# Reordering the attention stretch of a hybrid decoder trunk: feed-forward state opened before the first lead split, and one more weight tile

## The chip, the cores and the metric

The kernel runs on one core of a Trainium2 chip. The time of a kernel is the device time of one launch in microseconds (us), the median of several runs. Engines: PE (TensorE, matrix products and transposes), ACT (ScalarE), DVE (VectorE), POOL (GpSimd), and SP, whose queue issues the loads.

## What is computed

Two decoder layers over 256 tokens of width 1024, batch 1. Each layer is a feed-forward half-step, a token mixer, and a second feed-forward half-step; the first layer mixes with RWKV-7, the second with sliding-window attention over keys and values that are projected once between the layers. The part that matters here is the mixer of layer 1 and what joins it:

```python
D_MODEL = 1024; SEQ = 256; D_FF = 2816; Q_HEADS = 16; KV_HEADS = 4; WINDOW = BLOCK = 128

def swiglu(x, w_in, w_out):
    gate, up = jnp.split(x @ w_in, 2, axis=-1)
    return (jax.nn.silu(gate) * up) @ w_out

# swa_sinks: two query blocks of 128; scores against the previous and the own block of keys
q = (xq @ w_q + b_q).reshape(B, NB, BLOCK, KV_HEADS, GROUP, ATT_HEAD)
s = jnp.einsum('bnqkgd,bnskd->bnkgqs', q, kb) * (ATT_HEAD ** -0.5)
s = jnp.where(valid, s, MASK_VALUE)
p = softmax(concatenate([s, sink]))[..., :-1]
o = jnp.einsum('bnkgqs,bnskd->bnqkgd', p, vb)
return o @ w_o + b_o

# the layer
h = h + 0.5 * rms_norm(swiglu(rms_norm(h, g[0]), ...), g[1])
m = swa_sinks(rms_norm(h, g[2]), ...)
h = h + rms_norm(m, g[3])
h = h + 0.5 * rms_norm(swiglu(rms_norm(h, g[4]), ...), g[5])
```

## The kernel before

All activations stay on the chip; the weights, some 180 MB, are streamed once. Tokens are two halves of 128 (the number 0 or 1 in a unit's name). A weight chunk is 128 x 1024 in float32 (512 KB). `stream` loads it into one of four raw buffers (`wr`), ACT casts it to fp32r (the high part, L195), and DVE subtracts (the low part, L201); a product of two such pairs is three matmuls (`mm3`, L227). The split chunk lies in one of 11 slots in rotation (`W3`, `W1`, `W2`), and waits for the last product that used the slot 11 chunks ago.

The attention stretch is `att_region`. It is written as units, Python generators that emit a few instructions a step; the string `ATT` (L48) is the order in which the steps are taken, and `in_order` ties the instructions of PE, DVE and ACT to that order, each engine by itself. Loads are not tied, and instructions of later parts of the program can be put between by the scheduler. The units:

- `e0`, `e1`: the rest of the previous feed-forward's down projection, four steps of 12 matmuls.
- `p0`, `p1`: norm after it, update of the residual h, statistics; `x0`, `x1`: normed input, transposed in two groups of four (L309), cast and split (L1297, L1299).
- `wq`, `wo`, `wl`: eight steps each, one chunk of the query weights, the output weights and the lead chunks of the next feed-forward. `gn`: three gain rows, and as the fourth step the opening of the next feed-forward (`ffn_begin(3, ...)`: new input tile, lead 2, no lead chunks yet).
- `q0`, `q1`: query projection, eight steps of six matmuls; `t0`, `t1`: its copy, transposes and bias into the tile `qT`.
- `s00` to `s11` (query block, key head pair): scores (L1348), mask, maximum, exponentials (L1366, L1368), sums, division; `v00` to `v11`: probabilities transposed (L1388), copied, times values (L1397), split.
- `o0`, `o1`: output projection, eight steps of six; `r0`, `r1`: bias (L1268), square (L1271), gain (L1272), root on POOL (L239, L242), update of h (L1279), its squares (L1281); `z0`, `z1`: like `x0`, `x1`, for the next feed-forward.
- `l0`, `l1`: the first two blocks of the next feed-forward for one half: four steps of six matmuls for a block, Silu (L1441), multiply (L1443), a turn of two transposes (L1450), split. An `l` step asks `lead_chunk` for its chunk, which streams it if no `wl` step has.

Of `leads` it matters that `range(self.lead)` is taken at its first step, and that `lead_chunk` streams nothing for a chunk that is already in `self.wlead`. While the attention stretch begins, both still belong to the feed-forward before (`ffn_begin(2, xt, 1)`: lead 1, chunk (0,0) present). In the order before, the first `wl` stands ahead of the fourth `gn`.

After the stretch `ffn_main` runs the other blocks of the feed-forward (L362, L363: pairs of matmuls of 512 and 256 columns).

Of the kernel before, what the change touches and what calls it, by code (L numbers as in the profile page):

```python
# [9 lines left out]
F32R = mybir.dt.float32r  # L10
# [6 lines left out]
P = 128  # L17
D = 1024
# [27 lines left out]
PO = [(True, -3, 7), (True, -4, 2), (False, -1, 3), (True, -1, 7), (False, -3, 4), (True, -4, 2), (True, -1, 6), (False, -1, 6)]  # L46
P3 = [(False, 0, 0)] * 3 + [(False, x, 2) for x in (-4, -4, -4, -3, -3, -1, -1)]
ATT = """  # L48
wq wq e0 e0 p0 e0 e0 e1 e1 wq p0 p0 wq wq wq p0 p0 p0 p0 p0 x0 x0 e1 e1 p1 p1
p1 x0 x0 x0 x0 x0 q0 x0 p1 p1 p1 p1 q0 q0 q0 wq q0 q0 p1 wq x1 x1 wo wo wo x1  # L50
x1 x1 q0 q0 t0 t0 t0 t0 t0 gn t0 s00 s00 s00 s01 s01 s00 s01 x1 x1 s00 s00 s01 x1 q1 q1
s01 q1 q1 q1 wo q1 s01 s00 s00 s00 wo s01 s01 s00 s00 s01 q1 gn q1 wo t1 t1 t1 v00 t1 s01
v00 v00 t1 t1 s10 v00 v00 v01 s10 s01 v01 v01 s10 s10 v00 v00 s10 s10 s10 s11 s10 s10 s11 s10 s11 s11
s10 v01 s11 s11 v01 v01 s11 v01 o0 s11 s11 o0 o0 wo s11 s11 s10 s10 s10 o0 o0 o0 o0 wo s10 s10
o0 r0 v10 s11 s11 s11 v10 v10 v10 gn v10 v10 v10 v10 r0 r0 v10 v10 s11 s11 v10 r0 r0 wl v11 v11
v11 v11 v11 v11 v11 v11 o1 o1 v11 r0 r0 r0 r0 r0 v11 v11 gn z0 z0 wl o1 o1 o1 wl z0 wl
z0 z0 wl o1 o1 o1 r1 r1 z0 z0 l0 l0 r1 r1 r1 z0 l0 r1 r1 r1 r1 r1 z1 z1 l0 l0
l0 wl z1 z1 z1 z1 z1 l0 wl wl l0 l0 l0 l1 l1 l0 l0 l0 z1 l0 l1 l0 l0 l1 l1 l1
l1 l1 l1 l1 l1 l1 l1 l1
"""  # L60
TX1, TX2 = (6, 7), (6, 7)
# [16 lines left out]
class Trunk:  # L78
# [1156 lines left out]
    def att_region(self):  # L1235
        nc, a = self.nc, self.a
# [5 lines left out]
        wq, wo = self.resident(a["w_q"]), self.resident(a["w_ao"])  # L1242
# [177 lines left out]
        def leads():  # L1420
            for b in range(self.lead):
                for c in range(4):
                    self.lead_chunk(b, c)
                    yield

        def lead(i):
            for b in range(self.lead):
# [19 lines left out]
                if i == 0 or b == 0:  # L1447
# [6 lines left out]
                    yield  # L1454

        unit = {"wq": streams(wq), "wo": streams(wo), "gn": gains(), "wl": leads()}
        for i in range(2):
            unit.update({f"e{i}": t_end(i), f"p{i}": post(("p", i), i, lambda i=i: acc2[i], lambda: g_post, True),
# [163 lines left out]
```

## Time and profile before

| | us |
|---|---|
| median of 3 runs | 1054.13 (1053.63 to 1066.59) |
| profiled execution | 1054.67 |
| its span, first to last instruction | 1052.9 |
| PE busy in the span | 1024.4 |
| DVE busy | 699.4 |
| ACT busy | 564.9 |
| attention stretch, first `e0` to last `l1` product | 758.4 to 891.6 |

Times in the rows are us from the start of the span. A timeline row gives start, duration, engine, line, operation, out<-in with its shape and count, and in brackets how long the engine stood idle before it and for whom. Matmuls are pipelined and their ends are modelled, so a matmul's own duration is longer than its share of PE's time; the distance from one start to the next is what counts. The granted clock is the share of full TensorE speed: 1.00 is 2.4 GHz, 0.50 is 1.2 GHz.

### The profile page before, as it was taken

To read this page: it belongs to the slowest core of one execution; us is meant where nothing else is said; L and a number is where in the kernel's file an instruction comes from. 1 tells how busy PE (TensorE), PEld (TensorE's weight loads), DVE (VectorE), ACT (ScalarE), POOL (GpSimd) and SP (SyncE) were. 2 spreads that over 40 slices of the span, in tenths; PEclk is the share of its full clock that TensorE was granted. 3 is DMA by queue.
4 is the path that set the end of the run, shared out by engine and by line. 5 is a ranking of instruction groups with operands and counts; after the bars stand their busy time and mean duration, and the time that the engine had idled before them with its cause. 6 is when DMAs were issued, how large, how long until landed. Compare 5 with 4: busy or idle time off the path is not lost.

```text
span 1052.9 us, 16152 instructions
## 1 busy us (share of the span) xinstructions
PE 1024.4 (97%) x6264; PEld 860.9 (82%) x6264; DVE 699.4 (66%) x1125; ACT 564.9 (54%) x1014; POOL 20.5 (2%) x34
## 2 busy tenths in 40 slices
PE   6999999999999999999999999999999989999997
PEld 5888888779967887888888788888877668888886
DVE  6666655527798877766665676666668866765652
ACT  6655554365245546655455665555556755655541
POOL 0000000000000001000000000000010000000000
PEclk9999999999999999999999999999999989999999
DMA  8768664034354336766663386676535127766621
GB/s 285 242 195 279 221 193 168 24 117 142 120 171 132 124 134 206 260 199 205 196 184 124 114 268 215 205 241 190 179 111 169 41 82 258 244 216 191 189 81 40
DMA packets 52668, 183.04 MB, mean 174 GB/s; under 512 B 5744, under 2 KB 6000, under 8 KB 52464
## 3 DMA queue, kind: packets, MB, share of 16 engines
q1 hardware_dynamic: 52304, 181.49, 53.3%
q8 instruction: 49, 0.80, 0.3%
q10 hardware_dynamic: 288, 0.52, 0.1%
q14 instruction: 27, 0.22, 0.1%
HBM read 180.94 MB, written 1.05 MB: 173 GB/s over the span
## 4 chain that ended last, share of the span: by engine, by line
PE 90%; ACT 3%; DVE 3%; DMA 2%; issue 1%; POOL 0%; SPq 0%; DVEq 0%; POOLq 0%; ACTq 0%
PE bk L227 35%; PE bk L362 13%; PE bt L362 13%; PE bt L363 7%; PE bk L363 7%; PE bk L571 3%; PE bk L617 2%; PE bk L581 1%; ACT W L195 1%; DMA wr<-in_w_in_dram 1%; PE bc L1002 1%; PE bk L1053 1%; PE bt L309 1%; DVE W L201 1%; DMA wr<-in_w_in_lead_dram 1%
## 5 line engine op out<-in xcount | busy, mean ns | idle before, releaser
L201 DVE TENSOR_TENSOR W<-wr,W 128x1024 fp32r<-128x1024 f32 x280 | 341.1, 1224 | 190.1 <-ACT W L195 188.7
L195 ACT CAST W<-wr 128x1024 fp32r<-128x1024 f32 x280 | 291.9, 1049 | 189.9 <-issue 94.3
L227 PE MATMUL bk<-W,g2k 128*128 128x512 f32 x1056 | 246.0, 390 | 0.0
L227 PEld LDWEIGHTS bk<-W,g2k 128*128 128x128 f32 x1056 | 195.8, 188 | 40.1
L362 PE MATMUL bk<-xtl,W 128*128 128x512 f32 x296 | 105.1, 393 | 0.0
L362 PE MATMUL bt<-xtl,W 128*128 128x512 f32 x296 | 104.4, 391 | 0.3 <-DVE xtl L350 0.3
L362 PE MATMUL bt<-xth,W 128*128 128x512 f32 x296 | 104.5, 390 | 0.0
L362 PE MATMUL bk<-xth,W 128*128 128x512 f32 x296 | 104.3, 390 | 0.0
L363 PE MATMUL bt<-xth,W 128*128 128x256 f32 x296 | 83.5, 282 | 0.0
L363 PE MATMUL bk<-xth,W 128*128 128x256 f32 x296 | 83.5, 282 | 0.0
L363 PE MATMUL bk<-xtl,W 128*128 128x256 f32 x296 | 83.4, 282 | 0.0
L363 PE MATMUL bt<-xtl,W 128*128 128x256 f32 x296 | 83.4, 282 | 0.0
L227 PE MATMUL bk<-W,xtl 128*128 128x512 f32 x216 | 61.7, 434 | 6.4 <-ACT W L195 3.3
L362 PEld LDWEIGHTS bt<-xtl,W 128*128 128x128 f32 x296 | 55.6, 188 | 12.3 <-DVE xtl L350 0.7
L362 PEld LDWEIGHTS bk<-xtl,W 128*128 128x128 f32 x296 | 55.6, 188 | 12.2
L362 PEld LDWEIGHTS bk<-xth,W 128*128 128x128 f32 x296 | 55.6, 188 | 11.6
L362 PEld LDWEIGHTS bt<-xth,W 128*128 128x128 f32 x296 | 55.5, 188 | 11.6
L227 PEld LDWEIGHTS bk<-W,xtl 128*128 128x128 f32 x216 | 42.9, 204 | 20.3 <-ACT W L195 3.8
L363 PEld LDWEIGHTS bk<-xtl,W 128*128 128x128 f32 x296 | 55.8, 189 | 1.2
L363 PEld LDWEIGHTS bt<-xth,W 128*128 128x128 f32 x296 | 55.9, 189 | 0.1
L363 PEld LDWEIGHTS bt<-xtl,W 128*128 128x128 f32 x296 | 55.9, 189 | 0.1
L363 PEld LDWEIGHTS bk<-xth,W 128*128 128x128 f32 x296 | 55.9, 189 | 0.0
(287 smaller groups left out, 1374.7 us busy)
## 6 DMA issues: line engine op xcount, KB each, us to landing
wr<-in_w_in_dram SPq DMA_DIRECT2D x148, 512.0 KB, 3.9
wr<-in_w_out_dram SPq DMA_DIRECT2D x88, 512.0 KB, 3.6
wr<-in_w_in_lead_dram SPq DMA_DIRECT2D x28, 512.0 KB, 4.1
wr<-in_w_v_dram SPq DMA_DIRECT2D x16, 512.0 KB, 3.9
gain<-in_rows_dram SPq DMA_DIRECT2D x13, 512.0 KB, 4.5
wr<-in_w_k_dram SPq DMA_DIRECT2D x8, 512.0 KB, 4.1
wr<-in_w_r_dram SPq DMA_DIRECT2D x8, 512.0 KB, 3.6
wr<-in_w_o_dram SPq DMA_DIRECT2D x8, 512.0 KB, 4.3
```

The costliest lines, as they stand in the source:

```text
L195: self.follow(nc.scalar.copy(w[:, 0, :], raw), 0)
L201: self.follow(nc.vector.tensor_tensor(w[:, 1, :], raw, w[:, 0, :], op=ALU.subtract), 1)
L227: mm = lambda *x, **y: self.nc.tensor.matmul(*x, **y, **kw)
L309: t = self.nc.tensor.transpose(b[:, k * P:(k + 1) * P], xn[:, c:c + P], self.ident)
L362: mm(banks[j], hi[:, c0:c0 + P], xt[c][:, :, k4, :], start=(k == 0), stop=False)
L363: use[0] = mm(banks[j][:, 0:T], lo[:, c0:c0 + P], xt[c][:, 0, k4, :], start=False, stop=(k == KT - 1))
L571: self.nc.tensor.matmul(b[:, j * T:(j + 1) * T], ws[k // 4][:, c0:c0 + P], xf[:, k, :], start=(k == 0), stop=(k == KT - 1))
L581: nc.tensor.matmul(bs[j], l[:, k, j * P:(j + 1) * P], x[:, k, sl], start=(k == 0 and not e), stop=(k == KT - 1 and e == 1))
L617: mm(acc, x[:, 2 * k2 + k, :], w[:, k, :], start=(k2 + k == 0), stop=(k2 + k == 4))
L1002: mm(b[r, m * N:(m + 1) * N], W[r, v - hh * 16, :], XV[r, v, :], start=True, stop=True)
L1053: mm(out[hh][half[1 - e], m * N:(m + 1) * N], lhs, UV[part][:, hh * 16 + q, :], start=(not i and part == 0 and m == 0), stop=(part == e), ...
```

## The change

The list `ATT` is replaced by another order of the same 268 steps (each unit as often as before, apart from its place), and the first lead chunk, (0,0), is no longer split into a slot of the rotation but into the tile of the turned queries (`qT`, 128 x 2 x 1024, the same size). In the new list the fourth `gn` stands ahead of the first `wl`. As the diff, with the lines of the list in full:

```diff
 ATT = """
-wq wq e0 e0 p0 e0 e0 e1 e1 wq p0 p0 wq wq wq p0 p0 p0 p0 p0 x0 x0 e1 e1 p1 p1
-p1 x0 x0 x0 x0 x0 q0 x0 p1 p1 p1 p1 q0 q0 q0 wq q0 q0 p1 wq x1 x1 wo wo wo x1
-x1 x1 q0 q0 t0 t0 t0 t0 t0 gn t0 s00 s00 s00 s01 s01 s00 s01 x1 x1 s00 s00 s01 x1 q1 q1
-s01 q1 q1 q1 wo q1 s01 s00 s00 s00 wo s01 s01 s00 s00 s01 q1 gn q1 wo t1 t1 t1 v00 t1 s01
-v00 v00 t1 t1 s10 v00 v00 v01 s10 s01 v01 v01 s10 s10 v00 v00 s10 s10 s10 s11 s10 s10 s11 s10 s11 s11
-s10 v01 s11 s11 v01 v01 s11 v01 o0 s11 s11 o0 o0 wo s11 s11 s10 s10 s10 o0 o0 o0 o0 wo s10 s10
-o0 r0 v10 s11 s11 s11 v10 v10 v10 gn v10 v10 v10 v10 r0 r0 v10 v10 s11 s11 v10 r0 r0 wl v11 v11
-v11 v11 v11 v11 v11 v11 o1 o1 v11 r0 r0 r0 r0 r0 v11 v11 gn z0 z0 wl o1 o1 o1 wl z0 wl
-z0 z0 wl o1 o1 o1 r1 r1 z0 z0 l0 l0 r1 r1 r1 z0 l0 r1 r1 r1 r1 r1 z1 z1 l0 l0
-l0 wl z1 z1 z1 z1 z1 l0 wl wl l0 l0 l0 l1 l1 l0 l0 l0 z1 l0 l1 l0 l0 l1 l1 l1
+wq e0 e0 wq wq e0 e0 p0 p0 p0 e1 e1 e1 p0 wq p0 p0 p0 p0 x0 x0 wq wq x0 gn x0
+x0 e1 p1 p1 p1 p1 wo wq x0 x0 q0 x0 q0 q0 q0 q0 wo p1 p1 q0 wq p1 p1 wo q0 q0
+t0 t0 x1 x1 t0 t0 x1 x1 x1 t0 t0 s00 s00 s00 x1 s01 s00 s00 q1 q1 q1 s01 s00 x1 s01 s01
+q1 x1 s01 s01 wo s00 s00 q1 q1 s00 wo s00 s01 s01 s01 q1 q1 s01 t1 gn s01 t1 t1 t1 v00 s00
+v01 v01 t1 t1 gn v00 s10 s10 v00 s11 v00 v00 s10 v01 v00 s10 s11 v01 s10 v00 s10 v01 s11 s11 s10 s11
+s10 s10 s11 s11 s10 s11 s10 o0 o0 s11 v01 v01 s11 o0 o0 o0 wo o0 wo s11 o0 s10 s10 s10 wo o0
+s10 s11 s11 v10 v10 s10 v10 v10 v10 v10 v10 r0 v10 s11 r0 r0 v10 v10 s11 s11 v11 v11 v11 v11 gn v10
+v11 r0 v11 v11 v11 o1 r0 r0 v11 wl o1 o1 r0 r0 wl r0 r0 v11 o1 v11 o1 z0 z0 wl wl wl
+z0 z0 o1 z0 o1 wl o1 z0 r1 z0 l0 l0 r1 r1 z0 l0 r1 r1 r1 r1 l0 r1 l0 l0 l0 r1
+r1 z1 wl wl l0 l0 l0 l0 z1 z1 z1 z1 l0 l1 z1 l1 z1 z1 l1 l0 l0 l0 l0 l1 l1 l1
 l1 l1 l1 l1 l1 l1 l1 l1
 """
@@ leads()
             for b in range(self.lead):
                 for c in range(4):
-                    self.lead_chunk(b, c)
+                    if b + c == 0:
+                        w = self.tl("qT", [P, 2, D], F32R, tag="qT")
+                        self.wlead[0, 0] = self.stream(a["w_in_lead"][3, 0, 0], w)
+                    else:
+                        self.lead_chunk(b, c)
                     yield
```

## Rows read from the trace of the kernel before

**Rows 1.** The page: busy us, share, count; one load: count, KB, us to landing.
```profile
PE 1024.4 (97%) x6264; PEld 860.9 (82%) x6264; DVE 699.4 (66%) x1125; ACT 564.9 (54%) x1014; POOL 20.5 (2%) x34
...
wr<-in_w_in_lead_dram SPq DMA_DIRECT2D x28, 512.0 KB, 4.1
```

**Rows 2.** Windows: length, busy us (instructions) per engine, granted clock, DMA share, GB/s.
```profile
805.00:810.00 5.00, 4.20 (x18) 3.03 (x17) 3.54 (x13) 5.00 (x20) 0.00 (x0) 1.00 0.59 190
810.00:815.00 5.00, 4.31 (x31) 2.96 (x32) 4.52 (x12) 2.19 (x5) 0.00 (x0) 1.00 0.42 118
815.00:820.00 5.00, 4.52 (x33) 3.24 (x33) 4.92 (x10) 1.56 (x3) 0.00 (x0) 1.00 0.00 0
```

**Rows 3.** Waits of PE, 755 to 900: total us, times, longest.
```profile
PE bk L227 <- ACT W L195: 3.3, 2, 1.8
PE bt L309 <- ACT t L1322: 1.5, 1, 1.5
PE bk L227 <- DVE W L201: 1.4, 2, 0.8
```

**Rows 4.** Chain (first row) and timeline, 846 to 855, around the first lead product.
```profile
846.85 0.44 PE bt L309 x4
...
850.77 0.69 DVE L1268 TENSOR_TENSOR g2k<-bk,gain 128x512 f32<-128x512 f32 x1 [1.56 <-PE bk L227]
...
852.59 1.04 ACT L195 CAST W<-wr 128x1024 fp32r<-128x1024 f32 x1
853.67 1.22 DVE L201 TENSOR_TENSOR W<-wr,W 128x1024 fp32r<-128x1024 f32 x1 [1.48 <-ACT W L195]
...
853.69 0.66 PE L227 MATMUL bk<-W,xtl 128*128 128x512 f32 x1 [1.83 <-ACT W L195]
```

**Rows 5.** Timeline, 864 to 866, around the first product of lead block 1.
```profile
864.11 0.44 PE L1450 MATMUL bk<-cst,g2k 128*128 128x128 f32 x2
...
864.87 3.90 ACT L195 CAST W<-wr 128x1024 fp32r<-128x1024 f32 x4
...
865.99 0.49 PE L227 MATMUL bk<-W,xtl 128*128 128x512 f32 x1 [1.45 <-ACT W L195]
```

**Rows 6.** Windows of 1 us where the granted clock changes.
```profile
853.00:854.00 1.00, 0.31 (x1) 0.19 (x1) 0.33 (x1) 0.64 (x1) 0.00 (x0) 0.94 0.02 8
...
860.00:861.00 1.00, 1.00 (x5) 0.76 (x4) 0.68 (x2) 0.70 (x1) 0.29 (x1) 0.65 0.00 0
...
867.00:868.00 1.00, 0.75 (x2) 0.63 (x3) 1.00 (x2) 1.00 (x2) 0.00 (x0) 0.77 0.00 0
...
870.00:871.00 1.00, 1.00 (x3) 0.77 (x3) 1.00 (x2) 0.19 (x1) 0.00 (x0) 0.53 0.94 356
```

**Rows 7.** PE: three timeline rows, and one group of lines from 878 to 886.
```profile
826.30 5.61 PE L227 MATMUL bk<-W,xx 128*128 128x512 f32 x24
...
847.04 4.38 PE L227 MATMUL bk<-W,xx 128*128 128x512 f32 x18
...
888.65 2.96 PE L227 MATMUL bk<-W,xth 128*128 128x512 f32 x12
...
L362 PE MATMUL bt<-xtl,W 128*128 128x512 f32 x8 | 2.8, 393 | 0.0
```

**Rows 8.** Timeline: table loads and what follows; the second half's norm; Silu.
```profile
800.50 1.28 ACT L1366 ACT_TABLE_LOAD   x1
...
801.80 0.21 ACT L1366 ACTIVATE st<-st 128x8 f32<-128x8 f32 x1
...
856.28 0.16 DVE L239 SCALAR_TENSOR_TENSOR rs<-ss 128x1 f32<-128x1 f32 x1
...
857.17 1.41 DVE L1279 SCALAR_TENSOR_TENSOR h<-t,rs,h 128x512 f32<-128x512 f32 x2
858.02 0.63 ACT L1281 ACTIVATE t<-h 128x512 f32<-128x512 f32 x1 [1.77 <-DVE h L1279]
...
863.21 0.39 ACT L1441 ACTIVATE g2k<-bk 128x256 f32<-128x256 f32 x1 [2.51 <-PE bk L227]
```

## The prediction, made before the changed kernel was run

> **What bounds the kernel now.** I read the busy table of the page first: TensorE (PE) is busy 97% of the span [rows 1], so a new order of the same work can only take back what PE loses. The windows of 5 us over the attention stretch say where it stands still: 0.80, 0.69 and 0.48 us in three windows from 805 to 820, 2.0 together [rows 2]. The list of waits has the larger part, which lies after 850: twice for ACT's cast of a weight chunk (3.3 us) and twice for DVE's low half of one (1.4); the 1.5 for copied queries lies at 809 [rows 3]. The timeline shows what is late. The output projection of the second half ends at 851.42 (847.04 + 4.38) [rows 7]; call such an end E. After it PE has four transposes and then the first product of lead block 0, whose chunk (0,0) is cast only at 852.59: PE waits 1.83, does one product, and waits again for the low half [rows 4]. The same happens to chunk (1,0), cast at 864.87 after PE had begun its last ready work at 864.11 [rows 5]. The reason is in the list: the first `wl` comes before the fourth `gn`, so `leads()` counts with the old lead of 1 and loads (0,1), (0,2), (0,3) alone; five of the eight chunks are split inside the `l0` steps that multiply them.
>
> The waits cost more than their length. The granted clock is at 0.50 (1.2 GHz) from 853.9, 2.0 us after PE ran out, until 860.7, after it had worked on since 855; and again from 867.55 to 870.5 [rows 6]. After the wait of 1.5 us at 809 [rows 3] the windows stay at 1.00 [rows 2].
>
> **The change part by part.** Every unit keeps its number of steps, so the work is the same: 24 splits (16 for the two projections, 8 lead chunks), the same products, three gains, the same roots on POOL.
>
> *The opening, ahead of the splits.* The fourth `gn` now precedes the first `wl`, so all eight `wl` steps split. What does PE lose today from E on? Its last lead products end at 891.61 (888.65 + 2.96), 40.2 us after E; 5.6 of these are 16 pairs of the next feed-forward's products put between (two groups of 8, 2.8 us for one) [rows 7]: 34.6. The work in them is 96 products at 5.61/24 = 0.234 us [rows 7], 22.4; three groups of four transposes at 0.44 [rows 4], 1.3; three turns of two at half that, 0.7; together 24.4. So 10.2 us are lost, 4.7 in the four waits [rows 3], the rest at half clock and around the waits. In the new list `wl`.1 to `wl`.6 stand ahead of `l0`.1, and from the first of them PE has seven steps of the output projection and two groups of transposes before it, 42 x 0.234 + 0.9 = 10.7 us. ACT has listed there the six casts of 1.04 and some 3.2 other, 9.4; DVE six low halves of 1.22 [rows 4] and some 4.3 other, 11.6: it is 0.9 over, but the last two splits belong to block 1, which PE reaches 6 us later. They fit. `wl`.7 and `wl`.8 stand behind the second half's first norm; by the sums below DVE ends the low half of `wl`.7 at about E + 11.1 and PE asks for it at E + 11.3: zero, but each us of lateness there is paid by PE one to one. So 10.2 us can come back.
>
> *A new wait in its place.* In the new list PE's next step after the fourth product group of `l0` is the turn `l0`.7, with no transposes between, as there are now. It waits for Silu and multiply; behind it on PE stand the whole of block 1 and the second half. When is it ready? DVE has four low halves and a split (4 x 1.22 + 0.69 = 5.6 us) listed between the norm of the first half and the second half's bias add, so that add starts at about E (its input is there 0.65 earlier, 850.77 against 851.42 [rows 4, 7]). Two bias adds and a multiply, 3 x 0.69, to E + 2.0; a square and its sum, 0.85; DVE's split and multiply meanwhile, so the root begins on DVE at E + 3.3; from there to the update of h 0.89 (856.28 to 857.17), to the first square 0.85 (to 858.02), the square itself 0.7: E + 5.75 [rows 8]. Then the activation table for Silu, 1.28 as at 800.50, to E + 7.05, and from Silu to the turn 0.90 (863.21 to 864.11): E + 7.95 [rows 5, 8]. PE has 0.44 + 24 x 0.234 = 6.05 us until then and waits 1.9. Lower bound 0.9 (the load ends earlier, and only Silu to turn is left); upper 4.1 (the chain takes 7.9 us from bias add to the end of the first square as now, 850.77 to 858.7, instead of 5.75). I take 1.9. Behind Silu on ACT stand the second half's last square and the casts of `wl`.7 and 8; these set the E + 11.1.
>
> The second turn without cover, `l1`.7, is where pairs of the next feed-forward stand today; their inputs are ready by then, so I take zero (upper end 0.9).
>
> *The tile in the turned queries' place.* One load of 512 KB, one cast, one low half, as any chunk. The last score product (`s11`.6) stands 59 list places earlier, so the tile is free and costs nothing; the ring of 11 slots is relieved of one chunk. SP's queue holds nothing but loads, each waiting for its buffer; they keep their order except that (0,0) goes ahead of (0,1), and the gains wait for the same DVE steps as before. The projection steps ahead hide the load; without that cover it would cost PE up to its landing time, 4.1 us [rows 1], once.
>
> *The order from the tail to E.* Laid out by hand with the durations of the trace: the first half's input is turned one tail step sooner (PE has 84 products of tail work before it, and the norm chain needs about as long), 0; queries and second half's input, turned in alternation through two banks, +0.6; the 1.5 us wait at the second half's queries shrinks to about 0.7, since one cast less stands ahead of their copy; the output projection begins some 0.5 sooner; then ACT starts the second block's exponentials 1.1 us later and PE waits 0.5 to 0.9 more at its transposed probabilities. Sum about +0.2. Bounds: the 2.0 us of rows 2 gone, or as much again added.
>
> *Sum.* 10.2 - 1.9 - 0.2 = 8.1 us. The profiled execution took 1054.67 (span 1052.9 and 1.8 around it), 0.54 above the median of 1054.13; against it 1046.6, against the median 1046.0.
>
> **The rivals.**
>
> Clock: PE's new wait of 1.9 us lies between the 1.5 after which the clock stayed and the 2.0 after which it fell. If it falls, PE loses between half of 3.0 us (second fall) and half of 5.8 (first fall, less what PE stood still): 1047.5 to 1049.
>
> Table: after the load ACT stays empty for a while and Silu starts later. The rows speak against it: the load at 800.50 ends at 801.78 and the exponential starts at 801.80 [rows 8]. If ACT stood still once more as long as the load takes, 1.28 us: 1047.3. The Trainium skill, page "ScalarE: Activation LUTs", section "What ACT_TABLE_LOAD costs", has such a rule: besides some 1.28 us of load each switch costs about 1.38 of drain. By that figure the sum would be 6.7 us; no run here shows the drain.
>
> More gained: the wait at Silu at its lower bound and the 2.0 us of the score stretch gone: 1045 to 1043.
>
> Softmax gives part back, or the splits are late after all: DVE is busy 4.5 and 4.9 of 5 us from 810 to 820 [rows 2]; a delay of 3 to 7 us there gives 1049 to 1053. The first chunk late once more would cost its 2.4 us [rows 4] and 2.9 of clock: 1051.
>
> Other side: the exponentials of the second block are laid bare. In the new list the last cast of the output weights stands between the two groups, so 16 exponentials and that cast, some 9.5 us of ACT, end before the first copy of transposed probabilities. If the projection of the first half, which covers them, runs ahead by 8.1 us or more, nothing of the gain is left; at the full 9.5 the time is 1055.5, with a fall of the clock 1058. Against it: the same scores feed both, and by my layout ACT is late by 1.1, not by 8.
>
> **How the numbers follow.** Forecast 0.45 (own range 1044 to 1049: 2.0 us either way, and 0.9 at the second turn); clock 0.22; table 0.04; more gained 0.10; softmax or late splits 0.12; other side 0.07. The range 1043.0 to 1051.0 leaves out a little of "more gained", half of the softmax case and the other side, less than 2 in 10. A difference of 2% (21 us) is about what a measurement of this kernel can tell from no change; PE's losses in the stretch are 12 us, so faster by that has 0.02, slower (the other side, twice over) 0.02, within 0.96.
>
> **What would show it.** After the projection of the second half PE should go from the transposes into `l0` with no wait for a cast or a low half; one wait of about 1.9 us before a turn of two (L1450 today), with the table load just ahead of Silu; the granted clock at 1.00 throughout; and from E to the last lead product some 26.3 us plus any pairs put between. It is wrong if casts of lead chunks still stand behind E, if the clock falls after the turn, or if E itself moves by over 2 us.

## The result, and the profile after

The changed kernel takes 1046.72 us (median of 12 runs, 1045.41 to 1058.02) against 1053.88 for the kernel before in the same comparison (12 runs): a ratio of 0.9928, interval 0.9904 to 0.9951. The highest run of each kernel stands apart from the others, in the changed kernel at a mean clock of 0.987. The changed kernel's profiled span is 1045.0 us (before 1052.9), TensorE's granted clock 0.999 on the mean.

The page's busy line, to set against [rows 1]: PE has 4.3 us less of busy time for the same 6264 instructions.

```profile
PE 1020.1 (98%) x6264; PEld 857.6 (82%) x6264; DVE 698.0 (67%) x1125; ACT 564.2 (54%) x1014; POOL 19.6 (2%) x34
```

The list of PE's waits from 755 to 900 (total us, times, longest), to set against [rows 3]. The waits for casts of chunks (L195) and for their low halves (L201) are gone. A wait at the turn (L1454, L1450 before) has come, as forecast, and a second one that was not forecast: L1299 is the low part of the second half's transposed input, the unit `z1`.

```profile
PE bk L1454 <- DVE g2k L1447: 1.1, 1, 1.1
PE bk L227 <- DVE xtl L1299: 1.0, 1, 1.0
PE bt L309 <- ACT t L1322: 0.6, 1, 0.6
PE bt L309 <- DVE qT L1329: 0.4, 1, 0.4
PE bk L1348 <- DVE qT L1329: 0.3, 1, 0.3
```

Three windows around the softmax, and the two behind E in which PE stands still (columns as in [rows 2]). The clock's column shows 1.00 in each, where before it fell twice [rows 6].

```profile
805.00:810.00 5.00, 4.45 (x20) 3.24 (x18) 2.79 (x10) 5.00 (x22) 0.00 (x0) 1.00 0.58 174
810.00:815.00 5.00, 4.69 (x38) 3.54 (x38) 4.97 (x17) 2.09 (x4) 0.00 (x0) 1.00 0.09 36
815.00:820.00 5.00, 5.00 (x31) 2.46 (x30) 4.94 (x9) 2.34 (x4) 0.00 (x0) 1.00 0.00 0
855.00:860.00 5.00, 3.90 (x18) 2.89 (x17) 2.20 (x5) 4.57 (x8) 0.55 (x1) 1.00 0.00 0
865.00:870.00 5.00, 3.96 (x21) 3.13 (x20) 3.95 (x5) 3.27 (x5) 0.00 (x0) 1.00 0.93 333
```

The timeline from the end of the output projection on, to set against [rows 4, 5, 8]. E is 846.82 + 4.37 = 851.19.

```profile
846.82 4.37 PE L227 MATMUL bk<-W,xx 128*128 128x512 f32 x18
...
849.20 1.22 DVE L201 TENSOR_TENSOR W<-wr,W 128x1024 fp32r<-128x1024 f32 x1
...
850.55 0.69 DVE L1268 TENSOR_TENSOR g2k<-bk,gain 128x512 f32<-128x512 f32 x1
...
851.39 1.65 PE L227 MATMUL bk<-qT,xtl 128*128 128x512 f32 x6
...
855.41 0.63 ACT L1281 ACTIVATE t<-h 128x512 f32<-128x512 f32 x1 [1.92 <-DVE h L1279]
...
856.15 1.28 ACT L1445 ACT_TABLE_LOAD   x1
857.44 0.39 ACT L1445 ACTIVATE g2k<-bk 128x256 f32<-128x256 f32 x1
...
858.34 0.44 PE L1454 MATMUL bk<-cst,g2k 128*128 128x128 f32 x2 [1.10 <-DVE g2k L1447]
...
859.35 0.75 DVE L1291 SCALAR_TENSOR_TENSOR t<-h,rs,gain 128x512 f32<-128x512 f32 x1 [0.73 <-POOL rs L242]
860.02 4.63 DVE L201 TENSOR_TENSOR W<-wr,W 128x1024 fp32r<-128x1024 f32 x4
...
864.90 0.74 DVE L1291 SCALAR_TENSOR_TENSOR t<-h,rs,gain 128x512 f32<-128x512 f32 x1
865.56 0.69 DVE L1299 TENSOR_TENSOR xtl<-bt,xtl 128x512 fp32r<-128x512 f32 x1
...
866.30 1.21 PE L227 MATMUL bk<-qT,xtl 128*128 128x512 f32 x4 [1.04 <-DVE xtl L1299]
...
880.76 2.96 PE L227 MATMUL bk<-W,xth 128*128 128x512 f32 x12
```

Chunk (0,0), now in the tile `qT`, is multiplied at 851.39 straight behind the transposes, with no wait. PE then works up to the turn, which waits 1.10. Behind it DVE has four low halves in one group at 860.02: two are those of `wl`.7 and `wl`.8, the other two belong to chunks of the next feed-forward, which the scheduler put there (the list `ATT` ties only its own steps to each other). So `z1` is late, and PE waits 1.04 at 866.30.

The change is measured best in two stretches within one run, since the profiled starts of `e0` differ by 2.3 us from kernel to kernel while the code ahead of it is the same: from the start of `e0` to E, and from E to the end of the last lead product. The first row of `e0`, before and after:

```profile
758.38 21.94 PE L227 MATMUL bk<-W,g2k 128*128 128x512 f32 x96
...
759.09 19.22 PE L227 MATMUL bk<-W,g2k 128*128 128x512 f32 x84
```

Before, the two stretches are 93.04 and 40.2; after, 92.10 (851.19 - 759.09) and 32.53 (880.76 + 2.96 - 851.19), with 16 pairs of the next feed-forward's products among them in both. So the stretch gains 0.94 + 7.67 = 8.6 us; the medians differ by 7.2, with an interval of 5.2 to 10.1 from the ratio. The spans differ by 7.9, because `e0` began 0.7 later in the profiled run of after.

### The profile page after: what moved, and what is told of

It reads as the page before. It is cut to its first block, busy times and chain, and to the rows that moved or that the text cites. A ratio compares the mean times of both kernels' runs of the same rounds, so it can differ in the third digit from the quotient of the medians.

```text
span 1045.0 us, 16146 instructions
## 1 busy us (share of the span) xinstructions
PE 1020.1 (98%) x6264; PEld 857.6 (82%) x6264; DVE 698.0 (67%) x1125; ACT 564.2 (54%) x1014; POOL 19.6 (2%) x34
## 4 chain that ended last, share of the span: by engine, by line
PE 91%; DVE 3%; ACT 2%; DMA 2%; issue 1%; POOL 0%; SPq 0%; DVEq 0%; POOLq 0%; ACTq 0%
PE bk L227 35%; PE bk L362 13%; PE bt L362 13%; PE bt L363 7%; PE bk L363 7%; PE bk L571 3%; PE bk L617 2%; PE bk L581 1%; PE bt L309 1%; DMA wr<-in_w_in_dram 1%; PE bc L1002 1%; PE bk L1053 1%; PE bk L1397 1%; PE bk L1348 1%; ACT g2k L1368 1%
## 5 line engine op out<-in xcount | busy, mean ns | idle before, releaser
L201 DVE TENSOR_TENSOR W<-wr,W 128x1024 fp32r<-128x1024 f32 x279 | 339.7, 1224 | 185.8 <-ACT W L195 184.9
L195 ACT CAST W<-wr 128x1024 fp32r<-128x1024 f32 x279 | 290.8, 1049 | 188.9 <-issue 95.7
L362 PEld LDWEIGHTS bk<-xth,W 128*128 128x128 f32 x296 | 55.6, 188 | 11.6
L362 PEld LDWEIGHTS bt<-xth,W 128*128 128x128 f32 x296 | 55.5, 188 | 11.6
L227 PE MATMUL bk<-W,xtl 128*128 128x512 f32 x204 | 54.3, 412 | 0.8 <-DVE xtl L315 0.4
L227 PE MATMUL bk<-W,xth 128*128 128x512 f32 x216 | 54.0, 397 | 0.0
```

Source lines behind the costliest of these rows:

```text
L195: self.follow(nc.scalar.copy(w[:, 0, :], raw), 0)
L201: self.follow(nc.vector.tensor_tensor(w[:, 1, :], raw, w[:, 0, :], op=ALU.subtract), 1)
L227: mm = lambda *x, **y: self.nc.tensor.matmul(*x, **y, **kw)
L362: mm(banks[j], hi[:, c0:c0 + P], xt[c][:, :, k4, :], start=(k == 0), stop=False)
```

## The experiments

"Stretch" is the sum of the two parts just named, all from the one profiled run of each kernel. Each ratio is to the kernel before in the same comparison.

| kernel | `e0` to E | E to last lead product | stretch | median us | ratio and interval |
|---|---|---|---|---|---|
| before | 93.04 | 40.20 | 133.24 | 1053.88 | 1 |
| after | 92.10 | 32.53 | 124.63 | 1046.72 | 0.9928 (0.9904 to 0.9951) |
| e1_open_old | 93.04 | 31.41 | 124.45 | 1046.22 | 0.9930 (0.9917 to 0.9944) |
| e2_no_tile | 92.11 | 34.00 | 126.11 | 1047.42 | 0.9950 (0.9931 to 0.9968) |
| e3_open_late | 92.09 | 45.66 | 137.75 | 1059.70 | 1.0052 (1.0037 to 1.0066) |
| e4_turn_late | 92.16 | 32.52 | 124.68 | 1046.22, one run | |
| e5_norm_first | 92.09 | 32.53 | 124.62 | 1045.86, one run | |
| e6_hold3 | 92.10 | 33.93 | 126.03 | 1047.91, one run | |
| e7_hold6 | 92.08 | 36.51 | 128.59 | 1049.15, one run | |
| e8_all | 92.09 | 32.53 | 124.62 | 1047.88 | 0.9946 (0.9927 to 0.9966) |
| e9_all_pinned | 92.35 | 30.50 | 122.85 | 1044.04 | 0.9911 (0.9898 to 0.9925) |
| e10_pin_only | 92.08 | 31.76 | 123.84 | 1046.04 | 0.9936 (0.9917 to 0.9955) |
| e11_hold2 | 92.10 | 33.49 | 125.59 | 1047.20, one run | |

### Which part brings the gain: e1_open_old, e3_open_late, e2_no_tile

The theory of the prediction was that the opening alone brings the gain. The rival was that the new order, or the tile, brings a good part of it. e1_open_old is the kernel before with one step of `ATT` moved, the fourth `gn`:

```diff
-o0 r0 v10 s11 s11 s11 v10 v10 v10 gn v10 v10 v10 v10 r0 r0 v10 v10 s11 s11 v10 r0 r0 wl v11 v11
-v11 v11 v11 v11 v11 v11 o1 o1 v11 r0 r0 r0 r0 r0 v11 v11 gn z0 z0 wl o1 o1 o1 wl z0 wl
+o0 r0 v10 s11 s11 s11 v10 v10 v10 gn v10 v10 v10 v10 r0 r0 v10 v10 s11 s11 v10 r0 r0 gn wl v11 v11
+v11 v11 v11 v11 v11 v11 o1 o1 v11 r0 r0 r0 r0 r0 v11 v11 z0 z0 wl o1 o1 o1 wl z0 wl
```

> The order of before, with one edit: the fourth gn stands just ahead of the first wl, so that all eight lead chunks are split by wl steps; no chunk goes into the tile of the queries. Theory 'late splits' (mine): the gain comes from the opening, so the distance from E (end of the second half's output projection) to the last lead product falls from 40.2 us to between 32 and 34, casts of lead chunks stand ahead of their products, the granted clock stays at 1.00, and the time is 1045.5 to 1048. Rival 'order': the gain comes from the new places of the softmax and norm steps, and this kernel stays within 2 us of before. A mixture would lie between, near 1050.

It measured 0.993, as the whole change does, and from E (851.20) to the last lead product it takes 1.1 us less than the changed kernel. Three rows of PE's timeline of e1_open_old: the products of block 0 run without a break, one wait of 1.07 is left, for the normed input of `z1`, and the lead products end at 882.61.

```profile
851.39 3.04 PE L227 MATMUL bk<-W,xtl 128*128 128x512 f32 x12
...
858.30 1.29 PE L309 MATMUL bt<-cst,t 128*128 128x128 f32 x8 [1.07 <-DVE t L1291]
...
879.65 2.96 PE L227 MATMUL bk<-W,xth 128*128 128x512 f32 x12
```

e3_open_late is the other way round: the new order, with the fourth `gn` behind the first `wl` again, and (0,0) in the rotation of slots.

```diff
-s10 s11 s11 v10 v10 s10 v10 v10 v10 v10 v10 r0 v10 s11 r0 r0 v10 v10 s11 s11 v11 v11 v11 v11 gn v10
-v11 r0 v11 v11 v11 o1 r0 r0 v11 wl o1 o1 r0 r0 wl r0 r0 v11 o1 v11 o1 z0 z0 wl wl wl
+s10 s11 s11 v10 v10 s10 v10 v10 v10 v10 v10 r0 v10 s11 r0 r0 v10 v10 s11 s11 v11 v11 v11 v11 v10
+v11 r0 v11 v11 v11 o1 r0 r0 v11 wl gn o1 o1 r0 r0 wl r0 r0 v11 o1 v11 o1 z0 z0 wl wl wl
```

> The new order, with the fourth gn moved behind the first wl and no chunk in the queries' tile: the opening is undone, so that three chunks are split by wl steps and five inside the l0 steps, as before. Theory 'late splits': PE waits again for the cast and the low half of chunk (0,0) and of (1,0), 4 to 5 us in all, the clock falls to 0.50 at least once, and the time is 1052 to 1056. Rival 'order': the time stays within 2 us of the changed kernel, about 1047.

It is slower than the kernel before, by some 5.5 us as the ratio has it, and above the range that was expected. PE's waits of e3_open_late from 755 to 900, and three rows of its timeline:

```profile
PE bk L227 <- ACT W L195: 5.5, 3, 2.5
PE bk L227 <- DVE W L201: 2.5, 3, 1.1
PE bk L1450 <- DVE g2k L1443: 1.6, 1, 1.6
```

```profile
853.23 0.49 PE L227 MATMUL bk<-W,xtl 128*128 128x512 f32 x1 [1.62 <-ACT W L195]
...
870.81 1.05 ACT L195 CAST W<-wr 128x1024 fp32r<-128x1024 f32 x1 [5.44 <-DMA wr<-in_w_in_dram]
...
874.58 0.49 PE L227 MATMUL bk<-W,xth 128*128 128x512 f32 x1 [2.50 <-ACT W L195]
```

Three chunks are late, where before there were two. The third, at 874.58, is behind a new cause: on ACT its cast stands behind casts of the next feed-forward's chunks, and the first of these waits 5.44 us for its load. So the parts don't add up. In the stretch, the opening is worth 133.24 - 124.45 = 8.8 us in the old order, and in the new one 137.75 - 126.11 = 11.6; the new order costs 4.5 without the opening and 1.7 with it (e2 against e1), or 0.2 with the tile as well.

e2_no_tile asks what the tile does. It differs from the changed kernel only in that (0,0) takes a slot of the rotation:

```diff
-                    if b + c == 0:
-                        w = self.tl("qT", [P, 2, D], F32R, tag="qT")
-                        self.wlead[0, 0] = self.stream(a["w_in_lead"][3, 0, 0], w)
-                    else:
-                        self.lead_chunk(b, c)
+                    self.lead_chunk(b, c)
```

> The changed kernel, with the first lead chunk split into a slot of the rotation of 11 like the other seven. Theory 'late splits': the slot that it takes was freed in the query projection long before, so the time is that of the changed kernel within 0.5 us, 1046 to 1047.5. Rival 'slot': the tile in the queries' place is what lets the later chunks in early; then some later cast waits for a slot's last product, PE waits behind it, and the time is 1 to 4 us longer.

No cast of a lead chunk waits for a slot (from 800 to 873 no cast waits for a product of PE), and yet the profiled run loses 1.5 us of the stretch. The medians differ by 0.7, and the intervals of the two ratios overlap. The timeline of e2_no_tile around the turn:

```profile
855.47 1.05 ACT L195 CAST W<-wr 128x1024 fp32r<-128x1024 f32 x1 [2.21 <-DMA wr<-in_w_in_dram]
856.43 0.62 ACT L1281 ACTIVATE t<-h 128x512 f32<-128x512 f32 x1
...
857.16 1.28 ACT L1441 ACT_TABLE_LOAD   x1
...
859.35 0.44 PE L1450 MATMUL bk<-cst,g2k 128*128 128x128 f32 x2 [2.34 <-DVE g2k L1443]
...
859.54 4.59 PE L227 MATMUL bk<-W,xtl 128*128 128x512 f32 x12
```

A cast of the next feed-forward's chunk now stands on ACT ahead of the first square of the second half (855.47, where the changed kernel has the square at 855.41). Counted from E (850.97 here), the square comes 1.24 later (5.46 against 4.22), and so do table load and Silu; PE waits 2.34 instead of 1.10, and the clock falls: the 12 products behind take 4.59 instead of 3.04. What the tile is worth here is thus not space: in the profiled runs the compiled order of ACT happened to be a better one with it. No run moves that cast alone.

### What is left behind E: e4_turn_late, e5_norm_first, e10_pin_only, e8_all, e9_all_pinned

Two waits are left, 1.10 at the turn and 1.04 at `z1`. e4_turn_late takes the first turn two product steps later, so that Silu has cover:

```diff
+            late = None
...
+                    if late and c == 1:
+                        bt = self.bank()
+                        for m in range(2):
+                            nc.tensor.transpose(bt[:, m * P:(m + 1) * P], late[:, m, :], self.ident)
+                        yield
+                        gh, gl = (g[:, :, sl] for g in self.g[0])
+                        self.split(gh, gl, bt[:, 0:256].rearrange("p (m t) -> p m t", m=2))
+                        late = None
+                        yield
...
-                if i == 0 or b == 0:
+                if i == 0 and b == 0:
+                    late = sg
+                elif i == 0 or b == 0:
```

> The changed kernel, only the turn of block 0 of the first half moved two product steps later on PE. Theory 'latency': the 1.10 us wait is Silu, multiply and the way between the engines, nothing else, and goes away; what follows is reached 1.1 us earlier. Then the low half of the seventh lead chunk, ready at E + 10.0, is asked for at about E + 9.0, so PE waits some 0.8 there or, if not there, 1.5 to 2 instead of 1.04 for the low half of the second half's input: the time falls by 0.3 us at most. Rival 'one to one': nothing later is tight, E to the last lead product falls by 1.1 us.

It measured 32.52 behind E: nothing gained. The waits have moved, as its timeline shows: the low half of `wl`.7 is late by 0.81, `z1` by 1.28. The first row gives E, 850.64.

```profile
846.27 4.37 PE L227 MATMUL bk<-W,xx 128*128 128x512 f32 x18
...
860.75 1.43 PE L227 MATMUL bk<-W,xth 128*128 128x512 f32 x5 [0.81 <-DVE W L201]
...
865.75 1.20 PE L227 MATMUL bk<-qT,xtl 128*128 128x512 f32 x4 [1.28 <-DVE xtl L1299]
```

e5_norm_first takes the second gain step of `z1` on DVE ahead of the last two lead splits:

```diff
-r1 z1 wl wl l0 l0 l0 l0 z1 z1 z1 z1 l0 l1 z1 l1 z1 z1 l1 l0 l0 l0 l0 l1 l1 l1
+r1 z1 z1 wl wl l0 l0 l0 l0 z1 z1 z1 l0 l1 z1 l1 z1 z1 l1 l0 l0 l0 l0 l1 l1 l1
```

> The changed kernel, only the second normed half row of the second half moved ahead of the last two lead splits. If that row makes the low half of the second half's input late, the 1.04 us wait for it falls below 0.4 and E to the last lead product by some 0.7 us, less what the lead splits, now 0.7 us later, cost PE (0 to 0.5). If it is the two splits of the next blocks which stand between on DVE, the wait stays at 0.8 or more.

It came out between the two: the wait at `z1` fell to 0.61, one of 0.16 for a low half appeared, and the stretch behind E stayed at 32.53. Two rows of PE's timeline of e5_norm_first, the first for E (850.25):

```profile
845.88 4.37 PE L227 MATMUL bk<-W,xx 128*128 128x512 f32 x18
...
865.36 1.21 PE L227 MATMUL bk<-qT,xtl 128*128 128x512 f32 x4 [0.61 <-DVE xtl L1299]
```

The three kernels agree in one thing: PE goes on behind the wait for `z1` at E + 15.11 in each (866.30 - 851.19; 865.75 - 850.64; 865.36 - 850.25). In the changed kernel that instant is set by DVE, which works without a break from the first gain step, behind the root, at E + 8.16 (859.35) to the end of the low part at 866.25: gain, four low halves, the turn's low part, gain, low part. PE's wait at the turn lies inside this time and costs nothing by itself, as e4 shows. e10_pin_only tests it by taking away the two low halves of the next feed-forward alone, which may now stand on DVE only behind `z1`'s fifth step:

```diff
+        z1 = 0
         for nm in ATT.split():
             next(unit[nm], None)
+            z1 += nm == "z1"
+            if nm == "z1" and z1 == 5:
+                self.mark()
+        self.plan = [(False, len(self.st) - 1, 2)] * 4
```

> The changed kernel, and nothing else but that four splits of the next feed-forward's chunks may stand on DVE only behind z1.5, the second half's norm, where the compiled order of the changed kernel had put two of them between z1.1 and z1.2. Theory 'inserted splits': these two, 2.4 us of DVE, are what makes z1.5 late; PE's wait of 1.04 us for the copied low half of the second half's input goes, the wait of 1.1 us at the turn stays, and from E to the last lead product it takes 32.5 - 1.0 = 31.5 us; the median is 1046.7 - 1.0 = 1045.7. Rival 'DVE is full': the norm is late for the root and the listed lead splits ahead of it; the wait stays at 0.6 or more and the stretch at 32.0 to 32.5. Rival 'moved on': the two splits are late for the next feed-forward instead and PE waits about 1 us there, so the stretch is 31.5 and the median 1046.7.

The wait at `z1` is gone, and E to the last lead product falls to 31.76, 0.26 above the 31.5 expected, for a new wait of 0.27 at a cast of the same input. DVE's timeline of e10_pin_only shows two low halves between the gains and four behind the low part:

```profile
858.18 0.75 DVE L1291 SCALAR_TENSOR_TENSOR t<-h,rs,gain 128x512 f32<-128x512 f32 x1 [0.73 <-POOL rs L242]
858.86 2.35 DVE L201 TENSOR_TENSOR W<-wr,W 128x1024 fp32r<-128x1024 f32 x2
...
861.69 0.74 DVE L1291 SCALAR_TENSOR_TENSOR t<-h,rs,gain 128x512 f32<-128x512 f32 x1
862.88 0.69 DVE L1299 TENSOR_TENSOR xtl<-bt,xtl 128x512 fp32r<-128x512 f32 x1 [0.45 <-ACT xtl L1297]
863.49 4.62 DVE L201 TENSOR_TENSOR W<-wr,W 128x1024 fp32r<-128x1024 f32 x4
```

With the turn's 1.10 still there, this is near the best that the pin alone can do. e9_all_pinned joins the pin with the edits of e4 and e5 and takes `wl`.7 ahead of the seventh step of `r1`; e8_all is the same without the pin.

The edit of the list in both:

```diff
-z0 z0 o1 z0 o1 wl o1 z0 r1 z0 l0 l0 r1 r1 z0 l0 r1 r1 r1 r1 l0 r1 l0 l0 l0 r1
-r1 z1 wl wl l0 l0 l0 l0 z1 z1 z1 z1 l0 l1 z1 l1 z1 z1 l1 l0 l0 l0 l0 l1 l1 l1
+z0 z0 o1 z0 o1 wl o1 z0 r1 z0 l0 l0 r1 r1 z0 l0 r1 r1 r1 wl r1 l0 r1 l0 l0 l0 r1
+r1 z1 z1 wl l0 l0 l0 l0 z1 z1 z1 l0 l1 z1 l1 z1 z1 l1 l0 l0 l0 l0 l1 l1 l1
```

> The changed kernel with what its trace shows as still lost behind E taken away: the turn of block 0 stands two product steps later on PE (1.10 us of wait there now), the seventh lead chunk is split while ACT and DVE wait for the second half's norm, the second normed half row stands ahead of the last lead split, and the first splits of the next blocks stay behind the low half of the second half's first turned group (1.04 us of wait now). If PE's waits are paid one to one, both go and the time is 1.5 to 2.2 us under that of the changed kernel, with E to the last lead product at some 30.5 us in place of 32.5. If DVE's own chain sets the pace there, the waits move to the casts of the last lead chunk or to the norm, and the time is within 0.7 us of the changed kernel.

It came to 30.50 behind E and 1044.04 us, the lowest of all. That is 2.7 us under the changed kernel, where 1.5 to 2.2 was expected; the stretch is 1.8 shorter, and the intervals of the two ratios overlap. None of PE's waits behind E is left in the list from 755 to 900; what stands in it for e9_all_pinned lies at the turned queries and the first scores, ahead of E:

```profile
PE bt L309 <- ACT t L1322: 0.7, 1, 0.7
PE bt L309 <- DVE qT L1329: 0.5, 1, 0.5
PE bk L1348 <- DVE qT L1329: 0.3, 1, 0.3
```

> As the kernel with all four edits (E to the last lead product 30.5 us, median 1044.0), but without the one that holds the next feed-forward's first splits behind z1.5. If the inserted splits are a cost of their own, PE waits 0.6 to 1.3 us at z1.5 again, the stretch takes 31.1 to 31.8 us and the median is 1044.6 to 1045.3; if the other three edits alone removed the waits, the stretch stays at 30.5 and the median at 1044.0.

Here both accounts missed the size, though the first had the place. Without the pin the turn and the lead splits make no wait, and PE stands still once, for 2.36 us at `z1`: the gain of the three other edits is nothing, the stretch behind E 32.53 as in the changed kernel. DVE's group of four and PE's wait in e8_all:

```profile
859.88 4.62 DVE L201 TENSOR_TENSOR W<-wr,W 128x1024 fp32r<-128x1024 f32 x4
...
865.50 1.19 PE L227 MATMUL bk<-qT,xtl 128*128 128x512 f32 x4 [2.36 <-DVE xtl L1299]
```

PE goes on at E + 15.12 again (E is 850.38). The expected 0.6 to 1.3 did not count with DVE, which ends this wait: what is taken away ahead of it on PE only makes it longer. Nor did it count with the scheduler. The low half of `wl`.7 has left the group of four (DVE takes it at 854.42), and a third one of the next feed-forward has come into its place: ahead of `z1`'s low part DVE now has one low half more than in the changed kernel, and three more than in e9. So the chain is as long as it was. Pin and edits are worth 0.77 and 0.00 alone and 2.03 together.

### What the clock does behind such a wait: e11_hold2, e6_hold3, e7_hold6

The forecast left open whether the clock falls after the wait at the turn. These three lengthen it, with 2, 3 or 6 copies of 128 x 256 on ACT into a tile that nobody reads, ahead of the first Silu:

```diff
+                if i == 0 and b == 0:
+                    scr = self.pp.tile([P, 256], F32, name="scr", tag="scr")
+                    for _ in range(3):
+                        nc.scalar.copy(scr, L["g4"][:, 0:256])
                 nc.scalar.activation(sg, v[:, :, 0, :], AF.Silu)
```

> The changed kernel with two copies of 128x256 on ACT ahead of the first Silu, where three made PE wait 2.27 us and the clock fall, and none made it wait 1.10 us at full clock. The two take some 0.8 us, so PE waits about 1.85 us in either account. If such a wait is still free of the clock: the granted clock stays at 1.00, z1.5 waits 0.75 us less (1.04 to 0.3), and from E to the last lead product it takes about 32.5 us. If the clock falls: 3.1 to 3.3 us at half rate follow, the wait at z1.5 goes, and the stretch takes 32.5 + 0.75 + 1.5 - 1.0 = 33.7 us.

> The changed kernel with three small copies on ACT (128 x 256, into a tile that nothing reads) ahead of the first Silu, so that PE's wait at the turn of block 0 grows from 1.1 to about 2.2 us. Theory 'clock': a wait of PE of 2 us lets the granted clock fall to 0.50 for 3 to 6 us afterwards, so the time grows by 1.1 + 1.5 to 2.9 us. Rival: a wait of this length alone does not do it; the clock stays at 1.00 and only 1.1 us is lost.

> As the kernel with three small copies, with six: PE's wait at the turn grows to about 3.3 us. Both theories expect the clock to fall here; the price tells what a fall costs beside the wait: 2.2 us for the wait alone, 3.7 to 5.1 with a fall to 0.50 for 3 to 6 us.

The waits are 1.84, 2.27 and 3.58 us, and the clock fell to half rate behind each; the 12 products behind the turn take 4.58, 4.58 and 4.59 us, against 3.04 in the changed kernel. So a fall costs 1.5 us here, the same for a wait of 1.84 as for one of 3.58. A window of 1 us of e11_hold2 (columns as in [rows 2]), with the clock at 0.50 while PE is busy throughout:

```profile
859.00:860.00 1.00, 1.00 (x4) 0.80 (x3) 0.49 (x1) 1.00 (x2) 0.47 (x1) 0.50 0.00 0
```

In e11 and e6 the wait at `z1` is gone in turn, so that of 0.74 + 1.5 in e11 only 0.96 reach the end of the stretch (33.49 - 32.53), and of 1.17 + 1.5 in e6 only 1.40, which is under the 2.6 to 4.0 expected. In e7 a wait of 0.64 is left at `z1`, and 3.98 arrive.

## Why the prediction came out right, step by step

**The opening: right.** It gave 10.2 us as the loss behind E. With no wait left there e9 takes 30.50 where before it is 40.20, so 9.7 can be had, and e1 gets 8.8 of them with one step of the list moved. The six splits were in time, as the sum on ACT and DVE had it. The seventh was in time only because of the wait at the turn: in e4, where PE does not wait there, it asks for the low half of `wl`.7 at E + 9.3 and has it at E + 10.1.

**The wait at the turn: right in kind, too large.** 1.10 instead of 1.9. Its chain ended at E + 7.15 instead of E + 7.95, and most of that is its start. The sixth split's low half ends at 850.42, so the bias add of the second half begins at 850.55, E - 0.64 and not E: DVE was not 0.9 us over. From there the first square ends at 856.13, 5.58 after the bias add (5.75 in the sum); the table load takes 1.28, and from Silu to the turn are 0.90, both as forecast.

**No second wait: wrong.** The sum had nothing at `z1`; there PE waits 1.04. Its step "zero: they fit" laid out only the steps of the list, and the scheduler put two low halves of the next feed-forward, 2.4 us of DVE, in front of the second gain. e10 takes them away and 0.77 come back; e9, with the edits that this uncovers, 2.03. The sum also took each us of wait at the turn as paid; by e4, which removes that wait and gains nothing, it was not. So the 1.9 of the forecast's sum stood at the wrong place and was nearly the right size: 2.1 us of waits, ended by `z1`.

**The tile: right in what was forecast, and more.** It costs nothing and removes no wait for a slot. That the profiled run without it loses 1.5 us, with another order on ACT, was not foreseen.

**The order up to E: the wrong sign.** +0.2 was forecast, -0.94 measured, and between -0.88 and -0.96 in the ten kernels with this order other than e9, which has -0.69; why is not known. The row L1322 shows the piece forecast right (1.5 to 0.6 at the second half's queries); the 0.5 to 0.9 laid on the transposed probabilities did not come. Of the windows of [rows 2], 805 to 810 and the next two lost 2.0 us; in the profile after, the same windows lose 0.55, 0.31 and 0.

**Sum.** 8.1 was forecast, and 8.6 measured in the stretch: 9.7 to be had, less 2.03 left behind E, plus 0.94. The terms are off by -0.5, -0.1 and +1.1; the second is so small because too much at the turn and too little at `z1` cancel. The size of the mechanism that carries the forecast, 10.2 against 9.7, is no accident; that the whole came within half a us is in part luck. Against the medians 1046.0 was forecast and 1046.72 measured. From E to the last lead product, less the 5.6 of pairs put between, it takes 26.9 (26.3 forecast). Two lead chunks, `wl`.7 and `wl`.8, are still split behind E (two of the four low halves at 860.02); the prediction names that as a sign of being wrong, but its own sum had put them there. The interval of the ratio, some 0.2% to each side, tells a change of 0.7% from none, which the prediction thought took about 2%.

**The rivals.** The clock stayed at 1.00, so that rival did not come about. But behind a wait of 1.84 us, the size that was forecast, it fell (e11, 1047.2 us): with the wait as forecast, that rival would probably have been the case. That the wait came out shorter, and the clock stayed up, is luck. Its lower price was also misread: by the last row of [rows 6] (0.53 in the us from 870) the second fall lasts to 870.9 and not 870.5, so half of it is 1.7 and not 1.5. The table's is refuted: the load ends at 857.43 and Silu begins at 857.44. The Trainium skill, page "ScalarE: Activation LUTs", section "What ACT_TABLE_LOAD costs", adds some 1.38 us of drain to each switch. This trace does not show it: ACT stands empty for 0.02 us ahead of the load (856.13 to 856.15) and 0.01 behind it. "More gained" came about by half: the wait at the turn is near its lower bound of 0.9 and 0.94 of the 2.0 came back, but `z1` took 1.04. The exponentials were not laid bare: `e0` to E became shorter. The order without the opening is slower than before (e3), but because casts and low halves come late, not because of exponentials.

## What to carry to other kernels

When a stage's first operands are late, look for the step that decides how early their loads and splits are allowed to start; here one token of the list was worth the whole gain. A wait that is ended by another engine's unbroken chain can't be shortened by giving PE more cover ahead of it: e4 only moved it. Nor is it enough to take a step out of the chain while the scheduler may put another in: e8 did, and in e4, e5 and e8 alike PE went on at E + 15.1. Only the pin, which kept the inserted steps out, cut the chain. Read the chain in the compiled order, with the work of later stages that the scheduler puts into it, not in the order that was written.

## What the runs showed of the hardware

The length of a wait alone does not decide whether PE's clock falls. It fell after single waits of 1.84, 2.27, 2.34 and 3.58 us at the turn, and stayed at 1.00 after 2.36 us in the profiled run of e8_all, which is longer than three of these, and after 1.62 and 0.77 with one product between in e3 (where in the kernel before it fell after 1.83 and 0.60). Two windows of 1 us of e8_all, in the wait and behind it:

```profile
864.00:865.00 1.00, 0.00 (x0) 0.00 (x0) 1.00 (x3) 0.36 (x1) 0.00 (x0) 1.00 0.77 291
...
866.00:867.00 1.00, 1.00 (x8) 0.82 (x8) 0.94 (x1) 0.00 (x0) 0.00 (x0) 1.00 0.84 320
```

The median of e8_all is 1.9 us above its profiled run (1047.88 against 1045.97), near the 1.5 of a fall. That is what a fall behind the same wait in some runs and not in others would give; but only one run was profiled, so it stays open, as does what decides it.
